# A two-block network on one core: the order of steps in paired matrix products, buffers for sums, and the last products

## Chip, cores and metric
One core of a Trainium2 chip runs the whole program. The metric is the device time of one execution in microseconds (us), as the median of several runs; lower is better.

## What is computed
256 tokens of width 2048 pass through two blocks in 32-bit floats. Cut to what matters:

```python
# first block
h = rms_norm(x, norm_in_g); mem_n = rms_norm(mem, norm_mem_g)
qa, ka, va, za, qb, kb, vb, zb, qm, zm, gates = split(h @ w_in)       # w_in: 2048 x 17408
ya = causal_attention(rope(qa), rope(ka), va) * silu(za)              # 8 heads of 128
yb = dilated_mixture(rope(qb), rope(kb), vb) * silu(zb)               # 3 groups of 4 heads
ym = memory_attention(qm, mem_n @ w_mem_kv) * silu(zm)                # 4 heads of 256
g_a, g_b, g_m = split(sigmoid(gates))
merged = g_a * (ya @ w_proj_a) + g_b * (yb @ w_proj_b) + g_m * (ym @ w_proj_m)
x = rms_norm(x + merged @ w_out, norm_final_g)
# second block
u = rmsnorm(x, ln1); lru_x, lru_g, q, k, v, ret_g = split(u @ w_in_2) # 2048 x 6144
y = concat(rg_lru(conv(lru_x)) * gelu(lru_g), silu(ret_g) * groupnorm(retention(q, k, v)))
h = x + y @ w_out_2
u = rmsnorm(h, ln2)
out = rmsnorm(h + (silu(u @ w_gate) * (u @ w_up)) @ w_down, final)    # inner width 5632
```

With 256 tokens, nearly all of the work is products of a 256-row matrix with weights that are each read once, 418 MB in all.

## The kernel before
**Two floats per number.** TensorE multiplies rounded 32-bit floats. To keep accuracy, every operand is cut in two: `split` (L326 to L333) lets ScalarE write the rounded `hi` (L329) and VectorE the rest, `lo` = source - `hi` (L330). A product of two blocks is then three matmuls: hi x hi, lo x hi and hi x lo (L179 to L181 in `gemm`, L239 to L241 in `pair_gemm`). Left operands (activations, transposed to 128 x 256) are split once and kept; weights come by DMA into `raw` (three buffers of 1 MB), are split into `hi` and `lo` (four buffers each, of two 128 x 512 tiles), multiplied, and forgotten.

**Single products.** `gemm` makes 256 x 512 of output: two token halves of 128 rows, one PSUM bank each, over all rows of the weight. For each half step (two 128-row tiles of the weight) it does one `hi`, one `lo` and 12 matmuls of 512 columns, and then lets one piece of side work be issued.

**Paired products.** `pair_gemm` makes two such outputs at once from two column blocks a and b of the weights. A step takes 256 rows of both (a 1 MB `raw` tile). Seen in blocks, it is a 2 x 2 matrix (two token halves by two row tiles) times a 2 x 2 matrix (two row tiles by two column blocks). There are two kinds of steps:
- D: the eight block products as they are, 24 matmuls into four banks; two `hi`/`lo` pairs of whole tiles.
- S: seven products of sums of blocks, 21 matmuls into seven banks, by the scheme of Strassen and Winograd. VectorE first makes sums of weight blocks: `t13` (L274) and the two halves of `t24` (L275, L276); then four `hi`/`lo` pairs are split, from `raw`, `t13`, `t24`, and a half tile of `raw`. The sums of the left blocks are made once, when the left operand is made (`Lhs.put`, L160 to L170), and only for the steps that its string of kinds marks with S.

After the last S step (`i == s1`, L292), VectorE combines banks 1, 5, 6 and 7 (L294 to L298), and at the end adds banks 2, 4, 3 and 8 (L299 to L302). `STEPS` gives one string for each left operand, and every pair that uses this operand has its steps in just that order: `lx` (the first block's normalized input) DDSSDDDD, `u2` (the input of gate/up) DDSDSDSD, `ff` DDSDSDDD and `ff3` DDSDSD (the inputs of the down products: their inner width of 5632 is done in parts of 4, 4 and 3 times 512). The names of tiles in the profile are those of the products: `gu` is gate/up, `fd` down, `gate` the gates, `kza`, `qva`, `qm`, `zm`, `b` the other parts of `w_in`.

**Side work.** Attention, transposes and statistics are cut into pieces that wait in two queues (`later`, `soon`); `gemm` and `pair_gemm` issue one at certain points (`pair_gemm` only outside the stretch from the first to the last S step, since the eight banks are all in use there). For each of four heads `dilated_attention` (L689) has the pieces: scores of the first 128 queries, their transposes, scores of the second 128, their transposes (two pieces), values, finish. These run while `gate_one` makes the four `thg` tiles of the gates of the dilated branch.

**Buffers.** `slot` has 27 tiles of 4 KB a partition for everything that lives long. `w512` has eight 2 KB tiles. `prob` and `pt` have two 4 KB tiles each; these hold the attentions' probabilities and their transposes, and also `t13` and `t24`, and `fa` of `Lhs.put`.

**Order.** The program is written as a list of operations in Python; a scheduler turns it into one queue for each engine and may let a later operation pass an earlier one there. On the chip each queue runs in the order it was given, and semaphores hold an instruction back until its operands are there or its buffer is free.

**The end.** The last part of the down products (f0 = 8, `ff8` to `ff10`) makes c = 0 and 1 as a pair with two S steps, and c = 2 and 3 as single products; each c is added to `h1`, squared, and scaled by the last norm's weights.

Of the kernel before, what the change touches and what calls it, by code (L numbers as in the profile page):

```python
# [10 lines left out]
F32 = mybir.dt.float32  # L11
F32R = mybir.dt.float32r
# [39 lines left out]
def two_blocks(ctx: ExitStack, tc: tile.TileContext, x, xT, mem, memT, w_in, w_mem_kv, w_proj_a,  # L52
# [6 lines left out]
    sp = ctx.enter_context(tc.tile_pool(name="sp", bufs=NSLOT))  # L59
# [9 lines left out]
    def w512(name, shape=(P, 512)):  # L69
        return tp.tile(list(shape), F32, tag="w512", name=name, bufs=8)  # L70
# [52 lines left out]
    class Lhs:  # L123
# [24 lines left out]
        def put(self, i, src, gains=None, gain=None):  # L148
# [11 lines left out]
            a = tp.tile([P, 8, P], F32, tag="pt", name="fa")  # L160
# [10 lines left out]
    def gemm(name, w, r0, nk, col0, lhs, fine=False, tail=False, rate=1):  # L171
# [52 lines left out]
    def pair_gemm(name, wa, ca, wb, cb, lhs, r0=0):  # L224
        kinds = lhs.kinds
        n = len(kinds)
        s0, s1 = kinds.index("S"), kinds.rindex("S")
# [26 lines left out]
        for i, kind in enumerate(kinds):  # L254
            raw = wp.tile([P, 4, 512], F32, tag="raw", name="raw", bufs=3)
# [11 lines left out]
            if kind == "S":  # L267
# [4 lines left out]
                t13 = tp.tile([P, 2, 512], F32, tag="prob", name="t13")  # L272
                t24 = tp.tile([P, 2, 512], F32, tag="pt", name="t24")
                V.tensor_tensor(out=t13, in0=raw[:, 2:3].to_broadcast([P, 2, 512]), in1=raw[:, 0::3], op=ALU.add)  # L274
                V.tensor_tensor(out=t24[:, 0], in0=t13[:, 0], in1=raw[:, 3], op=ALU.add)  # L275
                V.tensor_tensor(out=t24[:, 1], in0=t24[:, 0], in1=raw[:, 1], op=ALU.add)  # L276
                for src, banks in ((raw[:, 0:2], "12"), (t13, "57"), (t24, "64"), (raw[:, 3:4], "3")):
                    hi, lo = parts(src, len(banks))
                    for m, b in enumerate(banks):
                        product(b, *form[b], hi[:, m], lo[:, m])  # L280
            else:
                for j, banks in enumerate(("24", "38")):
                    hi, lo = parts(raw[:, 2 * j:2 * j + 2])
                    order = [(b, k) for k in range(2) for b in banks]
                    if i == n - 1:
                        order.sort(key=lambda o: banks.index(o[0]))
                    for b, k in order:
# [846 lines left out]
```

## Time and profile before

| | before |
|---|---|
| median of 3 runs | 2211.64 us (2208.92 to 2212.5) |
| the profiled execution | 2211.25 us |
| its span, first to last instruction | 2209.5 us |
| TensorE busy | 2174.9 us, 98% |
| TensorE's weight loads (beside its matmuls) | 1790.1 us, 81% |
| VectorE busy | 1702.7 us, 77% |
| ScalarE busy | 1167.6 us, 53% |
| HBM | 418 MB read, 190 GB/s |
| granted TensorE clock, mean | 0.998 |

The profile is of one execution; the device time is longer than its span by what lies around the first and the last instruction. PE is TensorE, PEld its weight loads, DVE VectorE, ACT ScalarE, SP the engine that issues most DMAs. In a row of the timeline the first number is the start (us from the span's start), the second the duration; what stands in brackets is how long the engine stood idle before, and what ended it. Durations of matmuls overlap; their pace is the distance of two starts.

### The profile page before, as it was taken

How to read it: one execution, taken by the hardware profiler on the slowest of the kernel's cores; microseconds unless marked ns; L12 is line 12 of the kernel's file. 1: busy time of each engine (PE TensorE's matmuls, PEld its weight loads, DVE VectorE, ACT ScalarE, POOL GpSimd, SP SyncE). 2: the span in 40 equal slices, each digit the busy share in tenths (PEclk: the TensorE clock that was granted, in tenths of full speed). 3: DMA queues.
4: the chain of work that ended last, by engine and by line, in shares of the span. 5: the costliest groups of instructions: out<-in, count | busy, mean ns of one | idle time of the engine just before them, and what ended most of it. 6: DMA issues, size and time to landing. Idle time of an engine off the chain costs nothing.

```text
span 2209.5 us, 26102 instructions
## 1 busy us (share of the span) xinstructions
PE 2174.9 (98%) x9889; PEld 1790.1 (81%) x9889; DVE 1702.7 (77%) x2186; ACT 1167.6 (53%) x1452; POOL 9.2 (0%) x15
## 2 busy tenths in 40 slices
PE   8999999999999999999999999999999999999997
PEld 6888788788888888888888888888778888788776
DVE  5678778777678888556677777568998889988996
ACT  6755455555445555444554545555554555555553
POOL 0000000000000000000000000000000000000000
PEclk9999999999999999999999999999999999999999
DMA  8755465455565655446665545555555665565554
GB/s 305 250 187 191 144 208 174 172 171 190 191 210 175 220 196 178 158 149 215 213 212 184 177 153 173 188 172 191 191 190 192 207 202 182 191 211 188 191 196 147
DMA packets 219325, 421.80 MB, mean 191 GB/s; under 512 B 10816, under 2 KB 17088, under 8 KB 219200
## 3 DMA queue, kind: packets, MB, share of 16 engines
q1 hardware_dynamic: 218624, 419.09, 57.2%
q8 instruction: 77, 1.26, 0.2%
q10 hardware_dynamic: 576, 1.05, 0.1%
q14 instruction: 48, 0.39, 0.0%
HBM read 418.00 MB, written 2.10 MB: 190 GB/s over the span
## 4 chain that ended last, share of the span: by engine, by line
PE 86%; DVE 8%; DMA 3%; issue 1%; ACT 1%; SPq 0%; POOLq 0%; POOL 0%; ACTq 0%; DVEq 0%
PE gu L240 4%; PE gu L241 4%; PE gu L239 4%; DVE lo L330 3%; PE b L241 3%; PE b L240 3%; PE b L239 3%; PE wo L181 3%; PE wo L179 3%; PE wo L180 3%; PE gate L240 3%; PE gate L241 3%; PE gate L239 3%; PE fd L240 3%; PE fd L241 2%; PE fd L239 2%
## 5 line engine op out<-in xcount | busy, mean ns | idle before, releaser
L330 DVE TENSOR_TENSOR lo<-raw,hi 128x1024 fp32r<-128x1024 f32 x492 | 555.0, 1140 | 160.8 <-ACT hi L329 158.6
L329 ACT ACTIVATE hi<-raw 128x1024 fp32r<-128x1024 f32 x492 | 483.4, 995 | 369.0 <-PE gu L241 75.7
L201 DVE TENSOR_TENSOR lo<-raw,hi 128x1024 fp32r<-128x1024 f32 (+1 forms) x277 | 336.3, 1219 | 234.4 <-ACT hi L200 233.3
L200 ACT ACTIVATE hi<-raw 128x1024 fp32r<-128x1024 f32 (+1 forms) x277 | 291.9, 1056 | 349.8 <-PE wo L181 65.1
L329 ACT ACTIVATE hi<-t 128x1024 fp32r<-128x1024 f32 x146 | 154.5, 1058 | 177.3 <-DVE t L276 88.5
L330 DVE TENSOR_TENSOR lo<-t,hi 128x1024 fp32r<-128x1024 f32 x146 | 178.1, 1220 | 21.3 <-ACT hi L329 16.7
L274 DVE TENSOR_TENSOR t<-raw 128x1024 f32<-128x1024 f32 x73 | 89.0, 1220 | 26.0 <-DMA raw<-in_w_up_dram 15.5
L240 PE MATMUL gu<-lo,u20h 128*128 128x512 f32 x176 | 68.6, 390 | 0.0
L241 PE MATMUL gu<-hi,u20l 128*128 128x512 f32 x176 | 68.5, 389 | 0.0
L239 PE MATMUL gu<-hi,u20h 128*128 128x512 f32 x176 | 65.8, 395 | 0.0
L276 DVE TENSOR_TENSOR t<-t,raw 128x512 f32<-128x512 f32 x73 | 49.9, 684 | 0.3
L275 DVE TENSOR_TENSOR t<-t,raw 128x512 f32<-128x512 f32 x73 | 49.8, 683 | 0.1
L240 PE MATMUL gu<-lo,u22h 128*128 128x512 f32 x121 | 47.8, 395 | 1.3 <-DVE lo L330 1.1
L241 PE MATMUL gu<-hi,u21l 128*128 128x512 f32 x121 | 47.2, 390 | 0.0
L241 PE MATMUL gu<-hi,u22l 128*128 128x512 f32 x121 | 47.2, 390 | 0.0
L240 PE MATMUL gu<-lo,u21h 128*128 128x512 f32 x121 | 47.2, 390 | 0.0
L239 PE MATMUL gu<-hi,u22h 128*128 128x512 f32 x121 | 47.1, 389 | 0.0
L240 PE MATMUL gu<-lo,u23h 128*128 128x512 f32 x121 | 47.1, 389 | 0.0
L239 PE MATMUL gu<-hi,u23h 128*128 128x512 f32 x121 | 47.1, 389 | 0.0
L241 PE MATMUL gu<-hi,u23l 128*128 128x512 f32 x121 | 47.1, 389 | 0.0
L239 PE MATMUL gu<-hi,u21h 128*128 128x512 f32 x121 | 46.9, 399 | 0.0
L241 PEld LDWEIGHTS gu<-hi,u20l 128*128 128x128 f32 x176 | 33.0, 188 | 6.7
(1097 smaller groups left out, 5672.3 us busy)
## 6 DMA issues: line engine op xcount, KB each, us to landing
raw<-in_w_in_dram SPq DMA_DIRECT2D x240, 512.0 KB, 4.6
raw<-in_w_in_dram SPq DMA_DIRECT2D x64, 1024.0 KB, 5.2
raw<-in_w_gate_dram SPq DMA_DIRECT2D x88, 512.0 KB, 3.8
raw<-in_w_up_dram SPq DMA_DIRECT2D x88, 512.0 KB, 4.8
raw<-in_w_down_dram SPq DMA_DIRECT2D x76, 512.0 KB, 4.8
raw<-in_w_out_dram SPq DMA_DIRECT2D x32, 1024.0 KB, 5.1
raw<-in_w_mem_kv_dram SPq DMA_DIRECT2D x15, 1024.0 KB, 7.2
raw<-in_w_proj_m_dram SPq DMA_DIRECT2D x8, 1024.0 KB, 5.3
```

Of the source, the lines that this page charges most:

```text
L179: nc.tensor.matmul(ps[t], xh[:, c], hi, start=(kt == 0), stop=False)
L180: nc.tensor.matmul(ps[t], xh[:, c], lo, start=False, stop=False)
L181: nc.tensor.matmul(ps[t], xl[:, c], hi, start=False, stop=(kt == nk - 1))
L200: A.activation(hi[:, a:b], raw[:, h + a:h + b], AF.Copy)
L201: V.tensor_tensor(out=lo[:, a:b], in0=raw[:, h + a:h + b], in1=f32(hi[:, a:b]), op=ALU.subtract)
L239: nc.tensor.matmul(ps[b], xh, hi, start=first, stop=False)
L240: nc.tensor.matmul(ps[b], xh, lo, start=False, stop=False)
L241: nc.tensor.matmul(ps[b], xl, hi, start=False, stop=(left[b] == 0))
L274: V.tensor_tensor(out=t13, in0=raw[:, 2:3].to_broadcast([P, 2, 512]), in1=raw[:, 0::3], op=ALU.add)
L276: V.tensor_tensor(out=t24[:, 1], in0=t24[:, 0], in1=raw[:, 1], op=ALU.add)
L329: A.activation(hi, src, AF.Copy)
L330: V.tensor_tensor(out=lo, in0=src, in1=f32(hi), op=ALU.subtract)
```

## The change
The steps of a pair may stand in another order than the rows of its weights, and each product has a string of its own (`CFG`); of the left operand's string only the number of sums is left to it. The last 256-row steps with sums are taken for the S places of a string. `lx` gets sums for three steps; `qm`, `zm` and `ga` (gates of the causal branch) use all three, `qva`, `kza`, `gm` and `b` two of them, in the order DDSDSDDD; gate/up has its three S steps in the order DDSDSSDD. The last part of the down products has no S step and no pair; its `Lhs` makes no sums. `t13`, `t24` and `fa` get a tag of their own, `t4`, with three buffers; the attentions' `prob` and `pt` tiles come from the slots, now 29; `w512` has six tiles. The two additions of `t24` are written behind the first split of the step. In the dilated attention the scores of the second 128 queries are written ahead of the first transposes. The function `two` makes a pair where the string has an S, and two single products in turn where it is empty (`gb`, `wo`, `l`, `rv`, `rg`, `rqk`, `wo2`: single products before too).

```diff
-NSLOT = 27
-
-STEPS = {
-    "lx": "DDSSDDDD",
-    "u2": "DDSDSDSD",
-    "ff": "DDSDSDDD",
-    "ff3": "DDSDSD",
+
+CFG = {
+    "lx": "DDSDSDSD", "u2": "DDSDSDSD", "mg": "", "lu": "", "y2": "", "ff": "DDSDSDDD",
+    "qm": "DDSDSDSD", "zm": "DDSDSDSD", "qva": "DDSDSDDD", "kza": "DDSDSDDD", "gm": "DDSDSDDD", "ga": "DDSDSDSD",
+    "gb": "", "b": "DDSDSDDD", "wo": "", "l": "", "rv": "", "rg": "", "rqk": "", "wo2": "",
+    "gu": "DDSDSSDD", "fd": "DDSDSDDD",
 }
+SP = {"slot": 29, "w512": 6, "hl": 4, "t4": 3, "raw": 3}
...
+    def t4(name, shape):
+        return tp.tile(shape, F32, tag="t4", name=name, bufs=SP["t4"])
...
-    def pair_gemm(name, wa, ca, wb, cb, lhs, r0=0):
-        kinds = lhs.kinds
+    def pair_gemm(name, wa, ca, wb, cb, lhs, r0=0, kinds=""):
+
         n = len(kinds)
+        with_sums = [i for i in range(n) if lhs.kinds[i] == "S"][-kinds.count("S"):]
+        without = [i for i in range(n) if i not in with_sums]
+        order = [(with_sums if kind == "S" else without).pop(0) for kind in kinds]
...
-        for i, kind in enumerate(kinds):
-            raw = wp.tile([P, 4, 512], F32, tag="raw", name="raw", bufs=3)
+        for n_, kind in enumerate(kinds):
+            i = order[n_]
+            raw = wp.tile([P, 4, 512], F32, tag="raw", name="raw", bufs=SP["raw"])
...
-                t13 = tp.tile([P, 2, 512], F32, tag="prob", name="t13")
-                t24 = tp.tile([P, 2, 512], F32, tag="pt", name="t24")
+                t13 = t4("t13", [P, 2, 512])
+                t24 = t4("t24", [P, 2, 512])
                 V.tensor_tensor(out=t13, in0=raw[:, 2:3].to_broadcast([P, 2, 512]), in1=raw[:, 0::3], op=ALU.add)
-                V.tensor_tensor(out=t24[:, 0], in0=t13[:, 0], in1=raw[:, 3], op=ALU.add)
-                V.tensor_tensor(out=t24[:, 1], in0=t24[:, 0], in1=raw[:, 1], op=ALU.add)
                 for src, banks in ((raw[:, 0:2], "12"), (t13, "57"), (t24, "64"), (raw[:, 3:4], "3")):
+                    if src is t13:
+                        V.tensor_tensor(out=t24[:, 0], in0=t13[:, 0], in1=raw[:, 3], op=ALU.add)
+                        V.tensor_tensor(out=t24[:, 1], in0=t24[:, 0], in1=raw[:, 1], op=ALU.add)
                     hi, lo = parts(src, len(banks))
...
+    def two(name, wa, ca, wb, cb, lhs, key):
+
+        kinds = CFG[key]
+        if "S" in kinds:
+            yield from pair_gemm(name, wa, ca, wb, cb, lhs, kinds=kinds)
+        else:
+            yield gemm(name, wa, 0, KD, ca, lhs)
+            yield gemm(name, wb, 0, KD, cb, lhs)
...
     def prob_tile(name):
-        return tp.tile([P, 768], F32, tag="prob", name=name)
+        return slot([P, 768], name)
 
     def pt_tile(name):
-        return tp.tile([P, 768], F32, tag="pt", name=name)
+        return slot([P, 768], name)
...
-        later(key, lambda: scores(0), lambda: turn(0, 1), lambda: scores(1), lambda: turn(1, 0),
+        later(key, lambda: scores(0), lambda: scores(1), lambda: turn(0, 1), lambda: turn(1, 0),
               lambda: turn(1, 1), values, finish)
...
-    ths = [gate_one(1, c) for c in range(NCH)]
-    mg = Lhs()
+    ths = gate_pair(1, 0, "gb") + gate_pair(1, 2, "gb")
+    mg = Lhs(CFG["mg"])
...
     for f0, nf in parts:
-        ff = Lhs(STEPS["ff" if nf == 4 else "ff3"])
+        final = f0 + nf == 11
+        ff = Lhs("" if final else CFG["ff"])
         for f in range(f0, f0 + nf):
-            pg, pu = pair_gemm("gu", w_gate, f * 512, w_up, f * 512, lu2)
+            pg, pu = two("gu", w_gate, f * 512, w_up, f * 512, lu2, "gu")
...
-            if final and c >= 2:
+            if final or "S" not in CFG["fd"]:
                 ps = gemm("fd", w_down, f0 * 512, 4 * nf, c * 512, ff, tail=(c == NCH - 1))
             else:
                 if c % 2 == 0:
-                    both = pair_gemm("fd", w_down, c * 512, w_down, c * 512 + 512, ff, r0=f0 * 512)
+                    both = pair_gemm("fd", w_down, c * 512, w_down, c * 512 + 512, ff, r0=f0 * 512,
+                                     kinds=CFG["fd"])
                 ps = both[c % 2]
```

**VectorE where one gate/up pair ends and the next begins.** The first row is the last operation on the old pair's output; `lo<-raw,hi` splits weights, `fa`, `ff2l` and `ff2x` make a left operand for the down products, `t_` are `t13` and `t24` of the new pair's first S step. Before:

```order
L1044 SCALAR_TENSOR_TENSOR sg<-vv,hr_11733,sg 128x512
L330 TENSOR_TENSOR lo<-raw,hi 128x1024 x2
L167 TENSOR_TENSOR fa<-fa 128x128 x3
L330 TENSOR_TENSOR ff2l<-fa,ff2h 128x512
L167 TENSOR_TENSOR fa<-fa 128x128
L330 TENSOR_TENSOR ff2l<-trm,ff2h 128x512
L330 TENSOR_TENSOR lo<-raw,hi 128x1024
L330 TENSOR_TENSOR ff2x<-fa,ff2x 128x512
L274 TENSOR_TENSOR t_12934<-raw 128x1024
L330 TENSOR_TENSOR lo<-raw,hi 128x1024
L275 TENSOR_TENSOR t_12935<-t_12934,raw 128x512
```

And with the change:

```order
L1064 SCALAR_TENSOR_TENSOR sg<-vv,hr_11781,sg 128x512
L348 TENSOR_TENSOR lo<-raw,hi 128x1024 x2
L282 TENSOR_TENSOR t_12982<-raw 128x1024
L171 TENSOR_TENSOR fa<-fa 128x128 x3
L348 TENSOR_TENSOR ff2l<-fa,ff2h 128x512
L171 TENSOR_TENSOR fa<-fa 128x128
L285 TENSOR_TENSOR t_12983<-t_12982,raw 128x512
L348 TENSOR_TENSOR lo<-t_12982,hi 128x1024
L348 TENSOR_TENSOR ff2x<-fa,ff2x 128x512
L348 TENSOR_TENSOR ff2l<-trm,ff2h 128x512
L286 TENSOR_TENSOR t_12983<-t_12983,raw 128x512
L282 TENSOR_TENSOR t_13066<-raw 128x1024
```

Before, four splits stand between the last `sg` row and the first row of `t24` (L275), the fourth the S step's own; with the change there are two (L285 is the first row of `t24`), the second the S step's own. The other two have moved ahead of the `sg` rows: one split of the new pair stood there before, three do now.

**ScalarE in the first head of the dilated attention.** `probb,lb` is an exponential, `ptb<-trp` the copy of transposed probabilities, `thg` the gates. Before:

```order
L710 ACTIVATE probb,lb<-probb,nbb 128x384
L200 ACTIVATE hi<-raw 128x1024
L718 ACTIVATE ptb<-trp 128x384
L200 ACTIVATE hi<-raw 128x1024
L648 ACTIVATE thg<-gate,hr_x 128x512 x2
L710 ACTIVATE probb,lb<-probb,nbb 128x768
L200 ACTIVATE hi<-raw 128x1024
L718 ACTIVATE ptb<-trp 128x384
```

And with the change:

```order
L721 ACTIVATE probb,lb<-probb,nbb 128x384
L204 ACTIVATE hi<-raw 128x1024 x2
L721 ACTIVATE probb,lb<-probb,nbb 128x768
L729 ACTIVATE ptb<-trp 128x384
L204 ACTIVATE hi<-raw 128x1024
L729 ACTIVATE ptb<-trp 128x384
L658 ACTIVATE thg<-gate,hr_x 128x512 x2
L204 ACTIVATE hi<-raw 128x1024
```

The second exponential, which stood behind the first copy and the two `thg`, now stands ahead of both.

## Rows read from the trace of the kernel before

**Rows 1.** The page, busy time, share of the span and instructions of each engine.
```profile
PE 2174.9 (98%) x9889; PEld 1790.1 (81%) x9889; DVE 1702.7 (77%) x2186; ACT 1167.6 (53%) x1452; POOL 9.2 (0%) x15
```

**Rows 2.** Timeline of TensorE in a quiet stretch of gate/up (start, duration, instruction).
```profile
1541.63 0.39 PE L241 MATMUL gu<-hi,u21l 128*128 128x512 f32 x1
...
1544.13 0.39 PE L240 MATMUL gu<-lo,u22h 128*128 128x512 f32 x1
```

**Rows 3.** What the weight loader waited for: us in all, times, longest.
```profile
PEld gu L240 <- DVE lo L330: 8.9, 13, 1.5
PEld gu L239 <- ACT hi L329: 7.2, 13, 1.0
...
PEld fd L180 <- DVE lo L201: 4.3, 1, 4.3
PEld gate L239 <- ACT hi L329: 3.1, 5, 1.3
PEld trp L342 <- ACT probb L710: 2.9, 4, 2.1
...
PEld fd L239 <- ACT hi L329: 1.9, 4, 1.0
...
PEld kza L239 <- ACT hi L329: 1.7, 2, 1.5
PEld fd L240 <- DVE lo L330: 1.3, 3, 0.6
```

**Rows 4.** Timeline around one wait of gate/up.
```profile
1548.66 0.39 PE L239 MATMUL gu<-hi,u22h 128*128 128x512 f32 x1
...
1549.51 0.19 PEld L240 LDWEIGHTS gu<-lo,u22h 128*128 128x128 f32 x1 [0.88 <-DVE lo L330]
...
1549.85 0.40 PE L241 MATMUL gu<-hi,u22l 128*128 128x512 f32 x1
```

**Rows 5.** The page's costliest groups: VectorE's splits and sums (busy us, mean ns | idle before).
```profile
L330 DVE TENSOR_TENSOR lo<-raw,hi 128x1024 fp32r<-128x1024 f32 x492 | 555.0, 1140 | 160.8 <-ACT hi L329 158.6
...
L274 DVE TENSOR_TENSOR t<-raw 128x1024 f32<-128x1024 f32 x73 | 89.0, 1220 | 26.0 <-DMA raw<-in_w_up_dram 15.5
...
L276 DVE TENSOR_TENSOR t<-t,raw 128x512 f32<-128x512 f32 x73 | 49.9, 684 | 0.3
```

**Rows 6.** Timeline of VectorE ahead of the wait of rows 4.
```profile
1544.82 0.69 DVE L330 TENSOR_TENSOR lo<-raw,hi 128x512 fp32r<-128x512 f32 x1
1547.09 1.23 DVE L274 TENSOR_TENSOR t<-raw 128x1024 f32<-128x1024 f32 x1 [1.58 <-DMA raw<-in_w_up_dram]
```

**Rows 7.** Timeline of VectorE from the end of a gate/up pair to the next one's S step.
```profile
1564.00 0.68 DVE L300 TENSOR_TENSOR ww<-gu,ww 128x512 f32<-128x512 f32 x1
...
1568.43 2.35 DVE L330 TENSOR_TENSOR lo<-raw,hi 128x1024 fp32r<-128x1024 f32 x2
...
1578.45 0.68 DVE L276 TENSOR_TENSOR t<-t,raw 128x512 f32<-128x512 f32 x1
```

**Rows 8.** TensorE after its longest wait: timeline, and a window with the granted clock.
```profile
2167.78 0.63 PE L181 MATMUL fd<-hi,ff8l 128*128 128x512 f32 x1
...
2170.77 0.47 PE L179 MATMUL fd<-hi,ff8h 128*128 128x512 f32 x1
...
2167.40:2171.00 3.60, 3.60 (x10) 2.82 (x10) 3.50 (x4) 1.06 (x1) 0.00 (x0) 0.53 0.37 77
```

**Rows 9.** Timelines of TensorE and ScalarE in the first dilated head.
```profile
895.36 0.39 PE L181 MATMUL gate<-hi,hn3l 128*128 128x512 f32 x1
897.44 0.55 PE L342 MATMUL trp<-cst,probb 128*128 128x128 f32 x3 [1.69 <-ACT probb L710]
...
895.11 1.37 ACT L648 ACTIVATE thg<-gate,hr_x 128x512 f32<-128x512 f32 x2 [2.29 <-PE gate L181]
```

**Rows 10.** Gate/up and down as one window (PE, PEld, DVE, ACT, POOL busy); VectorE's waits for up weights.
```profile
1500.00:2135.00 635.00, 627.70 (x2781) 512.02 (x2780) 564.96 (x659) 349.41 (x384) 0.00 (x0) 1.00 0.59 193
...
DVE t L274 <- DMA raw<-in_w_up_dram: 15.5, 19, 1.8
```

More of the change, by code (lines that the diff above doesn't have):

```diff
@@ L283, in pair_gemm @@
                     hi, lo = parts(raw[:, 2 * j:2 * j + 2])
[L284 to L287, printed above, removed]
+                    todo = [(b, k) for k in range(2) for b in banks]
+                    if n_ == n - 1:
+                        todo.sort(key=lambda o: banks.index(o[0]))
+                    for b, k in todo:
                         product(b, *x(banks.index(b), k), hi[:, k], lo[:, k])
-                    if not s0 < i < s1:
+                    if not s0 < n_ < s1:
                         side()
-            if i == s1:
+            if n_ == s1:
                 p1, v, w, y = [w512(x) for x in ("p1", "vv", "ww", "yy")]
@@ L495, in two_blocks @@
         evac_T(ps, r_x, qmT[c])
[L496 removed]
+    for ps in two("zm", w_in, 10240, w_in, 10752, lx, "zm"):
         zm.append(evac_silu(ps, hr_x, "zm"))
@@ L516, in scores @@
             if i == 0:
-                st["pr"] = tp.tile([P, 2, NT, S], F32, tag="prob", name="probm")
+                st["pr"] = slot([P, 2, NT, S], "probm")
             for t in range(NT):
@@ L642, in gate_pair @@
         return ths
-    def gate_one(gcol, c):
-        ps = gemm("gate", w_in, 0, KD, 11264 + gcol * D + c * 512, lx)
-        th = slot([P, NT, 512], "thg")
-        for t in range(NT):
-            A.activation(th[:, t], ps[t], AF.Tanh, scale=hr_x[:, t:t + 1])
-        return th
     def project(c, th, w_proj, nk, lhs, first=False):
@@ L765, in two_blocks @@
         nc.sync.dma_start(gf, gfin_row[:, c * 512:(c + 1) * 512].to_broadcast([P, 512]))
-        ps = gemm("wo", w_out, 0, KD, c * 512, mg)
+        if c % 2 == 0:
+            both = two("wo", w_out, c * 512, w_out, c * 512 + 512, mg, "wo")
+        ps = next(both)
         x1c = slot([P, NT, 512], f"x1{c}")
@@ L891, in two_blocks @@
     hl = []
-    for c in range(2):
-        ps = gemm("lx", w_in2, 0, KD, c * 512, lu)
+    for c, ps in enumerate(two("lx", w_in2, 0, w_in2, 512, lu, "l")):
         need("rr")
@@ L995, in two_blocks @@
     h1 = x1
-    lu2 = Lhs(STEPS["u2"])
+    lu2 = Lhs(CFG["u2"])
     ss3 = small([P, NT, NCH], "ss3", 1)
     for c in range(NCH):
-        ps = gemm("wo2", w_out2, 0, KD, c * 512, y2)
+        if c % 2 == 0:
+            both = two("wo2", w_out2, c * 512, w_out2, c * 512 + 512, y2, "wo2")
+        ps = next(both)
         for t in range(NT):
```

73 lines of the change are left out of this document (38 added, 35 removed).

## The prediction
> **What bounds the kernel now.** The page comes first: TensorE is busy for 2174.9 of 2209.5 us, and no other engine is near that [rows 1]. So time can go in two ways only: fewer or faster matmuls, or fewer moments in which TensorE stands still. The second view is the timeline of TensorE in a quiet stretch, for the pace of a matmul that waits for nothing: eleven starts lie in 2.50 us, 0.227 us each [rows 2]. (The duration printed beside a start overlaps its neighbour; only the starts tell the pace.) The third view lists what TensorE's weight loader waited for [rows 3]. What a reader is to see there: after the kernel's first microseconds, nearly all waits are for `hi` (ScalarE) or `lo` (VectorE) of a weight, and nearly all of them in `gu`, `fd`, `gate` and `kza`, that is, in the paired products. These have two kinds of steps. A D step gives TensorE 24 matmuls, 24 x 0.227 = 5.4 us, and VectorE two subtractions of 1.22 us, 2.4 us [rows 5]: VectorE gains 3.0 us. An S step gives 21 matmuls, 4.8 us, and VectorE 1.22 (L274) + 2 x 0.68 (L275, L276) + 3 x 1.22 + 0.69 (a half tile) = 6.9 us [rows 5, 6]: VectorE loses 2.1 us. (The 1140 ns of the row of `lo<-raw` mixes whole and half tiles.) VectorE is therefore ahead on D steps, by at most the four `hi`/`lo` buffers, and is caught on S steps. In gate/up and down together it is busy for 565 of 635 us [rows 10]: enough in the mean, late in places.
>
> What one wait costs: at 1548.66 the next matmul starts after 0.85 us instead of 0.227, so 0.62 is lost, the one after it after 0.34, another 0.11; the row of the weight loader says 0.88 [rows 4]. So I take "row less 0.15" for each wait.
>
> The sums below stand against the profiled execution, 2211.25 us; the median of the three runs is 0.4 us above it.
>
> **A. Matmuls.** The queries' and memory gates' pairs (`qm`, `zm`, and both `ga`) get a third S step, four more; the last pair of down products, with two S steps, becomes two single products. Net two S steps more, each three matmuls fewer: TensorE has 8991 matmuls of 512 columns instead of 8997. 6 x 0.227 = **-1.4 us**. [...]
>
> **B. Last down products single.** The pair of c = 0, 1 leaves VectorE with eight operations to combine the banks and then the additions and scalings of four tiles, all ahead of the first `lo` of c = 2. That is the longest wait after the start: 4.3 us [rows 3], or 4.15 by the rule above. [...] With single products neither the banks' combination nor the sums of `ff8` to `ff10` are left, and VectorE does six subtractions (7.3 us) and four small operations in 72 x 0.227 = 16.3 us of matmuls for each c. Cover: if `ff10` came late, its 512 rows would be wanted after 48 matmuls (10.9 us) and not after 21 us as before; the transposes come in the second and third gap between half steps, 5.4 and 8.2 us in. That is tight but met. **-5.5 us**, bounds -5.6 and -3.5.
>
> **C. Waits in S steps.** Of rows 3, `gu` L240 and L239 (16.1 us, 26 waits), `fd` L239 and L240 (3.2, 7), `gate` L239 (3.1, 5) and `kza` L239 (1.7, 2): 24.1 us in 40 waits, less 40 x 0.15: 18.1 us. What the change does to them is three things.
> The order DDSSDDDD, with S at once behind S, goes from all pairs of the first block; every first S there has two D steps before it and one behind it. The tiles `t13` and `t24` no longer share two buffers each with the attention's `prob` and `pt`.
> In gate/up, DDSDSDSD becomes DDSDSSDD. At the end of a pair VectorE combines banks and makes `sg`, 1564.00 to 1568.43 [rows 7]. Before, one half step of the next pair is split ahead of that, and two more stand behind it (2.35 us at 1568.43 [rows 7]); TensorE reaches the first S step with VectorE still at its `t24` (1578.45) and waits. With two D steps at the end, the order on VectorE has three half steps ahead of the `sg` rows. VectorE then is 2 x 1.17 = 2.3 us further, more than the 1.5 us or so that one first S lost.
> Making `t24` behind the first `lo` costs and brings nothing by itself: the order before already has the first `lo` between `t13` and `t24`.
> Against it: S behind S now stands in each of the 11 gate/up pairs, 2 x 2.1 us against 3.0 gained on the D before it; and VectorE's wait for a weight's arrival in front of L274 (1.58 us at 1547.09, and 0.88 on TensorE behind it [rows 4, 6]) can come back before the second of the two, since its raw buffer is freed only when the first S of the pair is split. Bounds: 0 and -18.1. I take two thirds, the first-S waits and the first block's, and leave the rest: **-12 us**.
>
> **D. Dilated scores first.** In the first of four heads, the transposes of `probb` wait for its exponential, which stands behind two `thg` of 1.37 us on ScalarE: 895.36 to 897.44, 2.08 us for one matmul [rows 9], 1.85 lost. The others waited little (2.9 us in four waits [rows 3]). With both scores first, a half step of matmuls (2.7 us) lies between each exponential and its transposes, and the `thg` pair comes behind a copy of `ptb`. **-1.7 us**; bounds -1.85 and 0.
>
> **E. What is added.** Four S steps, each 2.1 us of VectorE's lead: 0 to 8.4 us; VectorE has 3.0 us spare in each of the five D steps of those pairs, so I take 1. The third set of sums of `lx`, made while `mk` and `mv` run without S steps, costs nothing; if that cover went, it is a few operations of 0.3 and 0.7 us. Two buffers fewer for 512-wide tiles and `prob`/`pt` out of the 29 slots can delay an evacuation; no row shows it, the nearest is the longest wait of `trp`, 2.1 us: from 0 to that, taken as 0 because `gu` uses just six such tiles (four banks, two `th`) and frees them before the next pair needs them. **+1 us**.
>
> Sum: -1.4 - 5.5 - 12 - 1.7 + 1 = -19.6; 2211.25 - 19.6 = 2191.7, and with the 0.4 of the median **2192 us**. A change under 0.2% (4.4 us) would not be told from none.
>
> **Rivals.**
> *The waits move.* S behind S in gate/up takes back what the first S gives: 11 pairs x (4.2 - 3.0) = 13 us at most, as much as `gu` lost in all (16.1 - 26 x 0.15 = 12.2). Then C is only `gate`, `kza` and `fd`, 8.0 - 14 x 0.15 = 5.9: -1.4 - 5.5 - 5.9 - 1.7 + 1 = -13.5, so 2198; and if these move too, 2204. For it: VectorE's share in that stage is unchanged, 89%. Against: half its loss came from lateness at a pair's end, which is mended.
> *Slower: additions stuck on arrivals.* With own buffers, L274 of a coming S step can stand further ahead in VectorE's queue and block splits behind it until its weights land. Before, 19 of 73 waited for an up weight, 15.5 us [rows 5, 10], 0.82 each; one shown cost TensorE 0.88 less 0.15 [rows 4, 6]. If all 33 S steps of gate/up did so with TensorE waiting each time, that is 27 us: with C lost, 2211.6 - 1.4 - 5.5 - 1.7 + 1 + 27 = 2231. It decides from about nine such waits (7.6 us) on: there the other terms are used up. [...] Against: splits that run ahead at a pair's start also free the raw tiles earlier, and with them the transfers.
> *Nothing gained.* Evacuations wait for slots or 512-wide tiles as long as the S steps wait less, C and D come to nothing and E to 3 to 8.4: 2211.6 - 6.9 + 3 to 8.4, or 2208 to 2213. The paired products of the first block would show it.
> *Everything gained.* All of C and D, none of E: -26.9, so 2185; a few waits not counted above (`om`, `lo` of `gate` and `kza`) would make it 2182.
>
> **How the numbers follow.** The forecast, with half to three quarters of C, 0.55 (2187 to 2197); moved waits 0.20 (2197 to 2205); everything 0.10 (2181 to 2187); nothing 0.08; slower 0.07. The range 2182 to 2205 leaves out the last two and a little of the fourth. Faster by over 0.2% (below 2207): the first three, 0.85; within 0.2%: 0.08; slower: 0.07.
>
> **What would show it.** Right: the wait of 4 us among the last down products is gone, and with it the stretch at half clock; `gu` under 6 us; no 2 us gap before `trp`; first S steps of gate/up without wait, the remaining ones at the second of the two S. Wrong: `gu` as long as before with its waits at step five (moved); VectorE's waits for up weights above 15.5 us (slower); new TensorE waits on ScalarE's or VectorE's evacuations in `qm`, `zm`, `qva` (slots). If the end of the trace shows a wait for `ff10`, term B was too large.

## The result and the profile after

| | before | changed |
|---|---|---|
| median, same comparison | 2211.1 us (2208.92 to 2212.5, 4 runs) | 2183.04 us (2181.7 to 2183.83, 4 runs) |
| the profiled execution | 2211.25 us | 2183.83 us |
| its span | 2209.5 us | 2182.0 us |

The ratio is 0.9873, with an interval of 0.9856 to 0.989: 28.1 us faster, where 19.6 was forecast. The range (2182 to 2205) holds it; the case that came true is the rival "everything gained".

First the page, busy times. It answers to [rows 1]: TensorE is busy 12.9 us less, in a span that is 27.5 us shorter, so at least 14.6 us of the gain are time in which it stood still. (Busy time understates it: a row lasts 0.39 us where the pace is 0.227, so the first part of each wait counts as busy.)

```profile
PE 2162.0 (99%) x9883; PEld 1789.9 (82%) x9883; DVE 1706.1 (78%) x2182; ACT 1171.5 (54%) x1453; POOL 9.2 (0%) x15
```

Next, of the same kernel, the waits of TensorE's weight loader (us in all, times, longest), all that are listed. They answer to [rows 3]:

```profile
PEld mk L183 <- ACT mn0h L350: 6.3, 1, 6.3
PEld qm L247 <- DVE lo L348: 2.7, 2, 1.5
PEld mk L184 <- DVE lo L205: 2.4, 3, 1.1
PEld mk L183 <- ACT hi L204: 1.9, 2, 1.3
PEld gate L246 <- ACT proba L608: 0.7, 2, 0.4
PEld trp L360 <- ACT proba L608: 0.7, 1, 0.7
PEld trq L360 <- PE rv L185: 0.5, 1, 0.5
PEld trq L360 <- DVE ra L465: 0.4, 1, 0.4
PEld kza L247 <- DVE lo L348: 0.3, 1, 0.3
PEld gate L247 <- DVE lo L348: 0.3, 1, 0.3
PEld gu L247 <- DVE lo L348: 0.2, 1, 0.2
PEld qva L247 <- DVE lo L348: 0.2, 1, 0.2
```

`fd` is gone altogether, and with it the one wait of 4.3 us; `gu` fell from 16.1 us in 26 waits to 0.2 in one; `gate` and `kza` on `hi` are gone; `trp` no longer waits for `probb`. What is new is `qm`, 2.7 us in two waits. Without the start-up (`mk`, which did not move), the whole list of before held 35.0 us in 54 waits; this one holds 6.0 in 11.

Two more rows of after: the stage of gate/up and down as one window (TensorE, its loads, VectorE, ScalarE, GpSimd busy; granted clock; DMA share; GB/s), and what VectorE's first addition waited for, by weight. They answer to [rows 10].

```profile
1500.00:2109.00 609.00, 609.00 (x2725) 503.93 (x2724) 555.87 (x641) 340.25 (x372) 0.00 (x0) 1.00 0.61 201
```

```profile
DVE t L282 <- DMA raw<-in_w_in_dram: 16.3, 15, 2.1
DVE t L282 <- DMA raw<-in_w_up_dram: 2.4, 4, 0.8
```

TensorE is busy for every one of 609 us, where before it missed 7.3 of 635. VectorE's wait for up weights went from 15.5 us to 2.4.

**Where the time came from.** I price the two lists with the prediction's own rule (a wait's row less 0.15 us):

- `gu`, `fd` (pairs), `gate` and `kza` on `hi`: 24.1 us in 40 waits became 0.2 in one, -18.05.
- the last down products: -4.15, and -1.4 for the slow stretch behind the wait: at a granted clock of 0.53 seven starts lie in 2.99 us [rows 8], 0.427 each, 0.2 above the pace.
- `trp` on `probb`: 2.9 us in four waits became none, -2.3.
- small ones that no term held (`om`, `gate` and `kza` on `lo`, `gate` L180, `trp` on `p`): 3.0 us in seven waits became 0.6 in two, -1.65.
- new: `qm` +2.4; `proba` and `qva` together +1.0 (1.6 us in four); `trq` +0.2.
- six matmuls fewer: -1.4.

The sum is -25.4. The profiled executions differ by 27.4, so some 2.0 us are not assigned to any row.

### The profile page after: what moved, and what is told of

Read it like the earlier page. It is cut to its first block, busy times and chain, and to the rows that moved or that the text cites. A ratio compares the mean times of both kernels' runs of the same rounds, so it can differ in the third digit from the quotient of the medians.

```text
span 2182.0 us, 26104 instructions
## 1 busy us (share of the span) xinstructions
PE 2162.0 (99%) x9883; PEld 1789.9 (82%) x9883; DVE 1706.1 (78%) x2182; ACT 1171.5 (54%) x1453; POOL 9.2 (0%) x15
## 4 chain that ended last, share of the span: by engine, by line
PE 95%; DMA 2%; DVE 2%; ACT 1%; issue 1%; SPq 0%; POOL 0%; POOLq 0%; DVEq 0%; ACTq 0%
PE gu L246 7%; PE gu L248 7%; PE gu L247 7%; PE b L248 3%; PE b L246 3%; PE b L247 3%; PE wo L183 3%; PE wo L185 3%; PE wo L184 3%; PE gate L246 3%; PE fd L246 3%; PE fd L248 3%; PE fd L247 3%; PE gate L248 3%; PE gate L247 3%; PE proj L185 2%
## 5 line engine op out<-in xcount | busy, mean ns | idle before, releaser
L347 ACT ACTIVATE hi<-raw 128x1024 fp32r<-128x1024 f32 x480 | 473.7, 993 | 391.5 <-PE gu L248 104.0
L348 DVE TENSOR_TENSOR lo<-raw,hi 128x1024 fp32r<-128x1024 f32 x480 | 541.8, 1139 | 132.2 <-ACT hi L347 127.7
L205 DVE TENSOR_TENSOR lo<-raw,hi 128x1024 fp32r<-128x1024 f32 (+1 forms) x289 | 351.0, 1221 | 239.8 <-ACT hi L204 238.6
L204 ACT ACTIVATE hi<-raw 128x1024 fp32r<-128x1024 f32 (+1 forms) x289 | 304.5, 1056 | 360.8 <-PE wo L185 65.1
L348 DVE TENSOR_TENSOR lo<-t,hi 128x1024 fp32r<-128x1024 f32 x150 | 183.1, 1222 | 28.1 <-ACT hi L347 26.6
L282 DVE TENSOR_TENSOR t<-raw 128x1024 f32<-128x1024 f32 x75 | 91.8, 1224 | 20.5 <-DMA raw<-in_w_in_dram 16.3
L246 PE MATMUL gu<-hi,u20h 128*128 128x512 f32 x176 | 70.3, 399 | 0.0
L286 DVE TENSOR_TENSOR t<-t,raw 128x512 f32<-128x512 f32 x75 | 51.7, 689 | 0.9
L285 DVE TENSOR_TENSOR t<-t,raw 128x512 f32<-128x512 f32 x75 | 51.6, 687 | 0.2
```

Source lines behind the costliest of these rows:

```text
L204: A.activation(hi[:, a:b], raw[:, h + a:h + b], AF.Copy)
L205: V.tensor_tensor(out=lo[:, a:b], in0=raw[:, h + a:h + b], in1=f32(hi[:, a:b]), op=ALU.subtract)
L246: nc.tensor.matmul(ps[b], xh, hi, start=first, stop=False)
L347: A.activation(hi, src, AF.Copy)
L348: V.tensor_tensor(out=lo, in0=src, in1=f32(hi), op=ALU.subtract)
```

## The experiments

Each edit is against the changed kernel, unless it says otherwise; each time is the median of four or five runs, and the ratio is to the kernel before, run beside it.

| | median (us) | ratio, interval | against changed | the same by the ratios |
|---|---|---|---|---|
| changed | 2183.04 | 0.9873, 0.9856 to 0.989 | | |
| u_gu | 2197.14 | 0.9935, 0.9922 to 0.9947 | +14.1 | +13.7 |
| only_gu | 2196.38 | 0.9942, 0.993 to 0.9955 | +13.3 | +15.3 |
| gu_3at_start | 2186.74 | 0.9895, 0.988 to 0.991 | +3.7 | +4.9 |
| u_buf | 2185.59 | 0.9883, 0.987 to 0.9897 | +2.5 | +2.2 |
| u_lx | 2183.62 | 0.9874, 0.9859 to 0.9889 | +0.6 | +0.2 |
| u_end | 2188.6 | 0.9897, 0.9884 to 0.9911 | +5.6 | +5.3 |
| u_dil | 2187.82 | 0.9902, 0.9887 to 0.9917 | +4.8 | +6.4 |
| u_t24 | 2183.02 | 0.9876, 0.9861 to 0.9891 | 0.0 | +0.7 |
| all3_gb | 2183.72 | 0.9882, 0.9866 to 0.9899 | +0.7 | +2.0 |
| all3 | 2173.56 | 0.9839, 0.9826 to 0.9853 | -9.5 | -7.5 |
| c_wo_w2 | 2173.72 | 0.9843, 0.983 to 0.9857 | -9.3 | -6.6 |
| c_wo | 2170.85 | 0.9831, 0.9818 to 0.9845 | -12.2 | -9.3 |

The last two columns differ because the kernel before, run beside each, took 2211.1 us (the runs u_gu, u_buf, u_lx, u_end), 2210.2 (gu_3at_start, u_dil, u_t24, all3_gb), 2208.6 (only_gu, all3, c_wo_w2) and 2208.2 (c_wo); why is not known. The text goes by the medians, since the traces bear them out: from the first `gu` matmul to the last, with the two `fd` stages between them, every execution in which no wait above 0.6 us falls there takes 635.3 to 635.8 us, in all four comparisons. Differences of 1 us between the rows of the table should not be read, and those across comparisons are good to some 3 us.

Undone one at a time (u_gu, u_buf, u_lx, u_end, u_dil, u_t24), the parts of the change add up to 27.6 of its 28.1 us.

### Gate/up in its old order: u_gu

```diff
-    "gu": "DDSDSSDD", "fd": "DDSDSDDD",
+    "gu": "DDSDSDSD", "fd": "DDSDSDDD",
```

> The changed kernel with one string put back: gate/up in the order DDSDSDSD. Theory 1 (the gain in gate/up comes from two D steps at a pair's end, so that VectorE is not late at the next pair's first S step): TensorE's waits in gu come back to 12 us or so, time 2193 to 2197. Theory 2 (it comes from t13 and t24 having buffers of their own): gu stays under 3 us of waits, time 2183 to 2186.

Measured: +14.1 us, with every other part of the change in place. The weight loader's waits of u_gu, first two rows:

```profile
PEld gu L247 <- DVE lo L348: 8.2, 14, 1.6
PEld gu L246 <- ACT hi L347: 6.4, 12, 1.0
```

That is the list of before again (16.1 us in 26 waits; here 14.6 in 26), though `t13` and `t24` have their own buffers. The timelines of VectorE show the shift that the prediction named. From the last `sg` row of a pair to the second half of the next pair's first `t24` (L286), in u_gu:

```profile
1559.97 0.75 DVE L1064 SCALAR_TENSOR_TENSOR sg<-vv,hr,sg 128x512 f32<-128x512 f32 x1
...
1564.91 1.23 DVE L348 TENSOR_TENSOR lo<-raw,hi 128x1024 fp32r<-128x1024 f32 x1
...
1567.78 1.23 DVE L348 TENSOR_TENSOR lo<-raw,hi 128x1024 fp32r<-128x1024 f32 x1
1568.91 0.70 DVE L285 TENSOR_TENSOR t<-t,raw 128x512 f32<-128x512 f32 x1
1569.52 1.23 DVE L348 TENSOR_TENSOR lo<-t,hi 128x1024 fp32r<-128x1024 f32 x1
1570.65 0.70 DVE L286 TENSOR_TENSOR t<-t,raw 128x512 f32<-128x512 f32 x1
```

and in the changed kernel:

```profile
1558.63 0.75 DVE L1064 SCALAR_TENSOR_TENSOR sg<-vv,hr,sg 128x512 f32<-128x512 f32 x1
1559.29 2.35 DVE L348 TENSOR_TENSOR lo<-raw,hi 128x1024 fp32r<-128x1024 f32 x2
1561.56 1.22 DVE L282 TENSOR_TENSOR t<-raw 128x1024 f32<-128x1024 f32 x1
...
1567.04 0.69 DVE L286 TENSOR_TENSOR t<-t,raw 128x512 f32<-128x512 f32 x1
```

`t24` comes 10.7 us after the last `sg` starts in u_gu, and 8.4 after it in the changed kernel: 2.3 us sooner, which is the two splits that now stand ahead of `sg` (in the first fence, at 1564.91 and 1567.78; each is 1.13 us to the next start). In u_gu TensorE's weight loader then waits for ScalarE's `hi` of that `t24`; in the changed kernel it does not wait at this boundary:

```profile
1572.55 0.19 PEld L246 LDWEIGHTS gu<-hi,u21x 128*128 128x128 f32 x1 [0.97 <-ACT hi L347]
```

From the first `gu` matmul to the last, u_gu takes 648.5 us and the changed kernel 635.4.

### Only gate/up in its new order: only_gu

This is the kernel before, with the new order in gate/up alone (and `t24` written behind the first split); buffers, the other pairs, the end and the dilated attention are the old ones.

```diff
-    "u2": "DDSDSDSD",
+    "gu": "DDSDSSDD",
```

(written here as an edit of the kernel before, and shortened; the run is the changed kernel with all other parts put back.)

> One part of the change alone: the kernel before with gate/up in the order DDSDSSDD (and t24's additions behind the first split); shared buffers, 27 slots, DDSSDDDD in the first block, the paired last down products and the old dilated order stay. If the order at the pair's boundary is the whole of gate/up's gain, and independent of the buffers: gu's waits under 1 us, 2211 - 14 = 2197. If it needs the own buffers too: gu waits of 4 us or more, 2201 to 2208.

Measured: 12.2 us faster than the kernel before (2208.55 beside it). `gu` is gone from the list of waits. So are the paired `fd` rows (3.2 us in seven), although the order of `fd` is the old one: those waits were gate/up's doing too. From the first `gu` matmul to the last it takes 635.3 us, where the kernel before took 649.8. The other large waits stand as in [rows 3]:

```profile
PEld fd L184 <- DVE lo L205: 4.3, 1, 4.3
PEld gate L246 <- ACT hi L347: 3.1, 5, 1.3
PEld trp L360 <- ACT probb L721: 2.9, 4, 2.1
```

One string of eight letters is 12 to 14 of the 28 us, and it needs none of the new buffers.

### Three D steps at the start: gu_3at_start

```diff
-    "gu": "DDSDSSDD", "fd": "DDSDSDDD",
+    "gu": "DDDSDSSD", "fd": "DDSDSDDD",
```

> The changed kernel with gate/up in the order DDDSDSSD: three D steps at a pair's start and one at its end, so that four D steps still lie between the last S of a pair and the first S of the next, and S behind S stays. If only their number counts (VectorE has 4 x 3.0 us there for the work at the boundary): gu waits under 3 us, 2183 to 2186. If it counts that two stand at the end (splits ahead of the banks' combination, before TensorE can wait for it): gu waits 8 us or more, 2191 to 2197.

Measured: +3.7 us, with this row in the list:

```profile
PEld gu L247 <- DVE lo L348: 2.5, 10, 0.9
```

From the last S step of a pair to the first of the next there are four D steps in both orders, three in the old one. That count is worth most of the 12 to 14 us; having two of the four ahead of the combination of banks, and not one, is worth the last 3.7. (The `gu` row is 1.0 us by the rule; `fd` waits again too, 2.0 us in five.) VectorE's timeline at the same boundary as in u_gu shows that the place of the splits is not the main thing:

```profile
1557.18 0.75 DVE L1064 SCALAR_TENSOR_TENSOR sg<-vv,hr,sg 128x512 f32<-128x512 f32 x1
...
1570.22 0.69 DVE L286 TENSOR_TENSOR t<-t,raw 128x512 f32<-128x512 f32 x1
```

Here `t24` comes 13.0 us after `sg`, later than in u_gu, and TensorE hardly waits, since it reaches its first S step one D step (5.4 us) later.

### Sums and attention in shared buffers again: u_buf

```diff
-SP = {"slot": 29, "w512": 6, "hl": 4, "t4": 3, "raw": 3}
+SP = {"slot": 27, "w512": 8, "hl": 4, "t4": 3, "raw": 3}
...
-                t13 = t4("t13", [P, 2, 512])
-                t24 = t4("t24", [P, 2, 512])
+                t13 = tp.tile([P, 2, 512], F32, tag="prob", name="t13")
+                t24 = tp.tile([P, 2, 512], F32, tag="pt", name="t24")
```

(`prob`, `pt` and `fa` take these two tags again as well.)

> The changed kernel with the buffers put back: t13, t24 and fa share two tiles each with prob and pt, 27 slots, eight 512-wide tiles; all orders stay changed. Theory 1: gu stays under 1 us of waits; only the pairs beside attention pieces (kza, gate) wait again, by up to 4 us: 2183 to 2188. Theory 2: gu's waits come back, 2193 or more.

Measured: +2.5 us. `gu` does not appear in the list; these do:

```profile
PEld gate L246 <- ACT hi L347: 2.0, 4, 0.7
PEld kza L247 <- DVE lo L348: 1.5, 2, 1.2
```

The buffers matter only where attention runs beside a pair, in the first block. (The edit puts back the numbers of slots and of 512-wide tiles as well; these were not tried apart.)

### The first block's pairs as before: u_lx

```diff
-    "lx": "DDSDSDSD", "u2": "DDSDSDSD",
+    "lx": "DDSSDDDD", "u2": "DDSDSDSD",
...
-    "qm": "DDSDSDSD", "zm": "DDSDSDSD",
+    "qm": "DDSSDDDD", "zm": "DDSSDDDD",
```

(likewise `qva`, `kza`, `gm`, `ga` and `b`; the own buffers stay.)

> The changed kernel with the first block's pairs put back: two sums of lx, all of its pairs in the order DDSSDDDD (buffers stay the tiles' own). 12 matmuls more: +2.7 us; the two new waits of qm (2.7 us on the list) go: -2.2. If the waits of kza and gate (5 us before) came from S behind S: they come back, 2187 to 2189. If they came from tiles shared with the attention: they stay away, 2183 to 2185.

Measured: +0.6 us, with 12 matmuls more, which are 2.7 us. Of `gate` and `kza` one wait of any size is left, so the old order did not make them:

```profile
PEld gate L247 <- DVE lo L348: 0.6, 1, 0.6
```

The wait of `qm` is absent here. So the four additional S steps, in the order that goes with them, save 2.7 us of matmuls and lose some 2.1 of it to waits; the four runs of the changed kernel lie 2.1 us apart, so it is not shown that they gain at all.

### The last down part as a pair: u_end

```diff
-        ff = Lhs("" if final else CFG["ff"])
+        ff = Lhs("DDSDSD" if final else CFG["ff"])
...
-            if final or "S" not in CFG["fd"]:
+            if final and c >= 2:
...
-                                     kinds=CFG["fd"])
+                                     kinds="DDSDSD" if final else CFG["fd"])
```

The question is whether the wait of 4.3 us [rows 3] and the slow stretch behind it [rows 8] come back.

> The changed kernel with the last part of the down products put back: a pair with two S steps (DDSDSD) for c = 0, 1. [...] If the wait was only VectorE being late from before, it is much shorter now: 2182 to 2184.

Measured: +5.6 us (2186.75 to 2191.2). The median, 2188.6, lies in the 2187 to 2189 that term B gives: 2183 + 5.5, with 1.0 for two waits in the pair's S steps and 1.4 less for six matmuls. The long wait is back, with its old length:

```profile
PEld fd L184 <- DVE lo L205: 4.3, 1, 4.3
```

The waits of the pair's own S steps did not come back. The edit takes six matmuls (1.4 us) away, so the wait and the slow stretch behind it cost 7.0. In the profiled execution the time from the last `gu` matmul to the last `fd` one is 71.4 us against 66.2, 6.6 us more when the six matmuls are counted: 4.15 for the wait, and an estimated 2.4 for 12 matmuls at the pace of [rows 8] (0.427 us, not 0.227), where the kernel before had seven.

### The old order of pieces in the dilated attention: u_dil

```diff
-        later(key, lambda: scores(0), lambda: scores(1), lambda: turn(0, 1), lambda: turn(1, 0),
+        later(key, lambda: scores(0), lambda: turn(0, 1), lambda: scores(1), lambda: turn(1, 0),
```

> The changed kernel with the dilated attention's first transposes again ahead of the second scores. My term D: a wait of about 2 us before trp in one head, 2184.5 to 2185. Rival (the wait came from the two gate evacuations standing ahead of the exponential, and the probabilities' tiles from the slots have changed that order already): no wait above 0.5 us, 2183.

Measured: +4.8 us. The row of the weight loader, and TensorE's timeline at the largest gap:

```profile
PEld trp L360 <- ACT probb L721: 3.9, 5, 2.5
```

```profile
891.42 0.39 PE L185 MATMUL gate<-hi,hn3l 128*128 128x512 f32 x1
893.93 0.55 PE L360 MATMUL trp<-cst,probb 128*128 128x128 f32 x3 [2.12 <-ACT probb L721]
```

2.51 us lie between the two starts, 2.3 more than the pace. By the rule the five rows are 3.2 us, and from the first `b` matmul to the first `wo` one u_dil takes 3.0 us longer than the changed kernel. The whole execution is 3.9 us longer; 1.3 of that lie ahead of the first `qm` matmul, where nothing was edited, and 0.4 is made up in between. In the changed kernel the same transposes follow at once:

```profile
890.41 0.39 PE L185 MATMUL gate<-hi,hn3l 128*128 128x512 f32 x1
890.64 0.49 PE L360 MATMUL trp<-cst,probb 128*128 128x128 f32 x3
```

### `t24` written ahead of the first split: u_t24

```diff
+                V.tensor_tensor(out=t24[:, 0], in0=t13[:, 0], in1=raw[:, 3], op=ALU.add)
+                V.tensor_tensor(out=t24[:, 1], in0=t24[:, 0], in1=raw[:, 1], op=ALU.add)
                 for src, banks in ((raw[:, 0:2], "12"), (t13, "57"), (t24, "64"), (raw[:, 3:4], "3")):
-                    if src is t13:
-                        V.tensor_tensor(out=t24[:, 0], in0=t13[:, 0], in1=raw[:, 3], op=ALU.add)
-                        V.tensor_tensor(out=t24[:, 1], in0=t24[:, 0], in1=raw[:, 1], op=ALU.add)
```

> The changed kernel with the two additions of t24 written ahead of the first split again. My reading (worth nothing by itself, since the order on VectorE had them behind the first split before too): 2182 to 2184, gu without waits. Rival (it is part of why the S steps do not wait): gu waits of several us, 2186 or more.

Measured: no difference (2183.02). This part of the change is worth nothing, as the prediction had it.

### More S steps with the cured boundary: all3_gb, all3

If the order at the end of a pair is the cure, three S steps in DDSDSSDD should pay in the first block too. all3_gb does that for all its pairs, and makes the dilated branch's gates as pairs as well; all3 leaves those gates single.

```diff
-    "qm": "DDSDSDSD", "zm": "DDSDSDSD",
+    "qm": "DDSDSSDD", "zm": "DDSDSSDD",
...
-    "gb": "", "b": "DDSDSDDD",
+    "gb": "DDSDSDDD", "b": "DDSDSSDD",
```

(`qva`, `kza`, `gm` and `ga` like `qm`; all3 keeps `"gb": ""`.)

> A version with more S steps: all pairs of lx with three of them, in gate/up's order DDSDSSDD, and the gates of the dilated branch as two pairs with two S steps. 45 matmuls fewer than the changed kernel: -10.2 us if TensorE waits no more than now: 2173. The two waits of qm (2.7 us on the list) should go, as there are two D steps at the pair's end: 2171. If VectorE has no room for the 15 more S steps (2.1 us of its lead each, up to 31 us): 2183 to 2200.

all3_gb failed: 2183.72 us with 45 matmuls fewer. That is a number of the last case above, but not for its reason, since it is not the S steps that wait. The wait that the dilated attention had lost is back, and larger:

```profile
PEld trp L360 <- ACT probb L721: 7.1, 4, 3.4
PEld trm L360 <- DVE yb L741: 1.3, 2, 0.6
```

A pair issues side work only outside the stretch of its S steps. The 28 pieces of the dilated attention do not fit into the 20 such points of two pairs; the remaining ones were issued back to back between 954 and 974 us, where each transpose waits for the exponential just ahead of it. From the first `b` matmul to the first `wo` one all3_gb loses 12.0 us against all3 (9.3 longer, with 12 matmuls fewer); these rows are 7.5 by the rule. Part of the rest is the clock, which was granted at 0.50 in two stretches (columns as above; the clock is the number before the DMA share):

```profile
958.33:961.74 3.41, 3.41 (x18) 3.41 (x18) 0.15 (x1) 0.98 (x2) 0.00 (x0) 0.50 0.57 220
968.57:971.98 3.41, 3.19 (x15) 3.19 (x16) 0.33 (x2) 1.53 (x5) 0.00 (x0) 0.50 0.00 0
```

TensorE had stood still for 3.20 us up to 958.14, and for 1.86 and 0.83 us up to 967.42 and 968.79. The 18 matmuls of values (`ob`) that begin in each of them took 3.32 and 3.06 us, and 2.17 in the changed kernel's first head. With the gates of that branch single again:

> The version with more S steps without the part that failed: all pairs of lx with three S steps in the order DDSDSSDD, the gates of the dilated branch single again. 33 matmuls fewer than the changed kernel: -7.5 us, and the two waits of qm gone: -2. VectorE has 4 x 3.0 us at each boundary, as in gate/up: 2173 to 2176. If VectorE or the side work (eight points of issue in a pair instead of ten) has no room: 2180 or more, with waits in b, kza or gate.

all3 measured 2173.56 us, 9.5 below the changed kernel. 33 matmuls fewer are 7.5 us at 0.227; its list beyond the start-up holds 3.3 us in six waits, against 6.0 in 11, so 2.0 less by the rule. That is the 9.5 of the medians; by the ratios it is 7.5.

### The output products as pairs: c_wo_w2, c_wo

all3, and `w_out` of the first block as pairs (c_wo), of the second block too (c_wo_w2):

```diff
-    "mg": "", "y2": "", "wo": "", "wo2": "",
+    "mg": "DDSDSDDD", "y2": "DDSDSDDD", "wo": "DDSDSDDD", "wo2": "DDSDSDDD",
```

(gathered in one line; c_wo has only `mg` and `wo`.)

> As before, and w_out and the second block's w_out as two pairs each with two S steps (DDSDSDDD): 24 matmuls fewer again, -5.4 us. VectorE is busy for 65% there, so room is not the question; the sums of their left operands, two more slots, and fewer points of issue are. If those cost nothing: 2168 to 2170. If the left operand comes late at the first S step, or the statistics' pieces are forced out together: 2173 to 2180.

c_wo_w2 gained nothing over all3 (2173.72 us) with 24 matmuls fewer. New waits took most of it (4.1 of 5.4 us by the rule), in the second block's product and at the start of gate/up behind it:

```profile
PEld gu L246 <- ACT hi L347: 2.9, 5, 1.4
PEld wo L246 <- ACT hi L347: 2.4, 3, 1.4
```

> The version with three S steps in every pair of lx, and the first block's w_out alone as two pairs with two S steps each (the second block's w_out, whose pairs waited 2.4 us at a late left operand and made the next gate/up wait 3.5, single again). 12 matmuls fewer than all3: -2.7 us, so 0.9827 of the kernel before, 2171 to 2173. If the pairs of w_out bring waits of their own (left operand late at the first S step, statistics forced out together): 0.984 or more.

c_wo has neither of these rows and measured 2170.85 us: 2.7 below all3 (1.8 by the ratios), as much as its 12 matmuls at 0.227. It is faster than both kernels of this case, by 12.2 us than the changed one (9.3 by the ratios).

## Why the prediction was right, and where not

**A, matmuls (-1.4).** Held. c_wo and all3 agree with 0.227 us for each matmul taken away, within what the medians can tell.

**B, last down products (-5.5).** Held: by the two lists and the stretch of [rows 8] it is 5.55, 4.15 and 1.4. u_end is no measure of its size: undoing the part costs 7.0 apart from the matmuls, above the bound of 5.6, because the slow stretch is longer there. The cover that the prediction named for `ff10` was there; the changed kernel has no wait in `fd` at all.

**C, waits in S steps (-12, bounds 0 and -18.1).** This is the term that was mis-sized: it came to -18.05, its outer bound. The step that failed is "I take two thirds", and behind it the remark that S behind S would leave waits at the second of the two. Each of the 11 gate/up pairs has S behind S, and one wait of 0.2 us is left.

The balance behind that remark, "2 x 2.1 us against 3.0 gained on the D before it", does not hold. It adds up VectorE's durations, which overlap as TensorE's do: in the fence of u_gu a split of 1.23 us is followed after 1.13, an addition of 0.70 after 0.61. With 1.13 and 0.60, an estimate for an S step is 4 x 1.13 + 3 x 0.60 = 6.3 us, so it loses 1.55, and a D step gains 3.2: two S steps cost just what the D step ahead of them gives.

The two thirds also took first S steps for too small a part. By the starts of TensorE's matmuls in the trace of before, `gu` lost 12.8 us around its S steps, 10.1 of it in the pairs' first ones and 2.7 in the D step behind the second; the prediction had about half come from lateness at a pair's end. And the paired `fd` waits, which it left standing in part, went with gate/up's order (only_gu).

That VectorE has a lead in the S steps can be seen: at the last of three, directly behind another, it waits 0.86 us for ScalarE's `hi` at 1538.10 in the changed kernel, and that `hi` had itself waited 0.73 us for a matmul of `gu` to be done with its buffer.

```profile
1538.10 1.23 DVE L348 TENSOR_TENSOR lo<-raw,hi 128x1024 fp32r<-128x1024 f32 x1 [0.86 <-ACT hi L347]
```

The prediction also left out that VectorE's own waits for up weights would shrink: 13 us less over 11 pairs is 1.2 us a pair, as much as that balance charged. That this helped is argued, not shown.

The shift at the boundary came as predicted, 2.3 us, with 2.3 in the two timelines. But gu_3at_start gets most of the gain without it: what counts first is that four D steps, and not three, lie between the last S step of a pair and the first of the next, which the prediction did not say. Of the first block's part the prediction gave two reasons, the order and the buffers. u_lx and u_buf tell them apart: with the old order and own buffers the waits of `gate` and `kza` are gone, with the new order and shared buffers they are there. It was the buffers (with the numbers of tiles that go with them), some 2.5 us.

**D, dilated scores (-1.7).** Right in kind, somewhat small: it was 2.3, outside its bound of 1.85, since all four waits of before went and not only the longest. Undoing it costs 4.8, of which some 3 belong to it: in the changed kernel's surroundings the same wait is longer (3.9 us in five rows, the longest 2.5). Why it grew there, and whether the tiles now taken from the slots have part in it, was not tried.

**E, what is added (+1).** `qm` pays 2.4 us in the profiled execution, and u_lx puts the price of the four extra S steps at some 2.1. The row of `qm` is 1.0 to 2.7 us in the seven executions that have this order in it, so 2.7 is its upper end; and only_gu, with the old order in `qm`, shows one wait of 1.7 us, some 13 us after an addition that had waited 3.5 us for its weight. The prediction's "3.0 us spare in each of the five D steps" did not cover the new ones. The timeline of VectorE in `qm` shows the mechanism of the rival on the slower side, at the later of the two waits:

```profile
124.69 1.23 DVE L282 TENSOR_TENSOR t<-raw 128x1024 f32<-128x1024 f32 x1 [1.83 <-DMA raw<-in_w_in_dram]
125.83 0.68 DVE L348 TENSOR_TENSOR lo<-raw,hi 128x512 fp32r<-128x512 f32 x1
126.43 0.69 DVE L285 TENSOR_TENSOR t<-t,raw 128x512 f32<-128x512 f32 x1
127.15 0.69 DVE L286 TENSOR_TENSOR t<-t,raw 128x512 f32<-128x512 f32 x1
127.76 3.49 DVE L348 TENSOR_TENSOR lo<-raw,hi 128x1024 fp32r<-128x1024 f32 x3
```

and the one of TensorE, what it costs:

```profile
129.04 0.50 PE L247 MATMUL qm<-lo,hn2h 128*128 128x512 f32 x1 [0.83 <-DVE lo L348]
```

An addition stands at the head of VectorE's queue until its weight lands (1.83 us), and the splits of the step ahead stand behind it. (Ahead of the earlier wait, 1.5 us at 117.67, an addition waited only 0.45 us for its weight, at 113.32.) All such waits for `w_in` are 16.3 us in 15 in the changed kernel; with two S steps everywhere in the order DDSSDDDD (u_lx) they are 5.6 in five. But all3, with three S steps in every pair and two D steps at the end, has 7.5 in ten, and of `qm`'s wait 0.4 us is left: it is the order, more than the number of S steps.

**The rivals.** "The waits move" fell with the 0.2 us of `gu`. "Slower" fell in gate/up (up weights 2.4 us, not above 15.5) and came true in small in `qm`. "Nothing gained" fell. "Everything gained" came true, and its second figure, 2182, also counted the small waits that did go. It had a chance of 0.10; what spoke for it was the prediction's own 2.3 us against 1.5, and the balance above, had it gone by starts. That the range still held the result, by 1 us, is in part luck: without the 2.6 us by which the new waits exceed E, it would have been 2180.4, below the range.

From -19.6 to -27.4: C -6.05, D -0.6, the small waits -1.65, B -0.05, the rest without a row some -2.0, less the 2.6 by which the new waits are above E.

## What to carry to other kernels

When a helper engine feeds a busy one and the mean shares fit, look at where the helper's extra work falls due (here the combination of a finished output), and put more of the steps that are light on the helper around that place; it was worth 12 to 14 us with no work removed, most of it by their number and the last 3.7 by having them on both sides. Make the helper's balance from the distances of starts, not from durations that overlap. Give short-lived sums a buffer of their own only beside work that uses the same buffers at the same time, since elsewhere that was worth nothing. Before a stage is made denser, count the points at which side work can still be issued in it: where they run out, the side work comes in a heap, and its waits can eat the gain.

## What was not expected of the hardware

The wait of 4.3 us in the last down products had the same length in u_end as before, but not the same aftermath. In the window of the slow stretch (columns as above; the granted clock is the number before the DMA share), only_gu, and then u_end:

```profile
2152.40:2155.80 3.40, 3.40 (x9) 2.62 (x9) 3.38 (x4) 1.06 (x1) 0.00 (x0) 0.50 0.29 86
```

```profile
2139.20:2146.00 6.80, 4.99 (x12) 3.93 (x13) 6.37 (x8) 1.07 (x5) 0.00 (x0) 0.50 0.36 88
```

In both the granted clock was 0.50. In only_gu it was still 1.00 when TensorE went back to work, at 2150.96, and was 0.50 for 3.4 us from 2152.40 (so too in the kernel before, [rows 8]: back to work at 2166.18, 1.00 up to 2167.40, 0.50 from 2167.80 to 2170.80); in u_end it was 0.50 while TensorE still waited, from 1.8 us before the first matmul at 2141.01, and for 6.8 us in all, 5.0 of them with matmuls. So the same wait is followed by 3.4 us of slow matmuls in one execution and by 5.0 in another. What decides it was not tried. The four runs of u_end lie 4.5 us apart, those of the changed kernel 2.1.
